# Join of the experts in a two-layer block: gated rows on VectorE and TensorE, two late experts

## The chip, the cores and the metric

One core of a Trainium2 chip runs the whole program; the other cores are idle. The metric is the device time of one execution in microseconds (us). The engines are named as in the profile: PE is TensorE's matmul stream and PEld its weight loads, DVE is VectorE, ACT is ScalarE, POOL is GpSimd, SP is the engine that issues most DMAs.

## What is computed

Two layers of a transformer block on 512 tokens of 1024 channels, in float32. Each layer has attention, a layer norm, a mixture of 16 experts of which every token uses two, and a second layer norm:

```python
x = layer_norm(ALPHA * x + mix, ln1_g[l], ln1_b[l])
ffn = grouped_moe(x, ...)       # sum over a token's two experts: gate * (silu(x Wg) * (x Wu)) Wd
x = layer_norm(ALPHA * x + ffn, ln2_g[l], ln2_b[l])
```

The change lies in the last two lines: how the expert rows of a token are added up, and the second layer norm on that sum.

## The kernel before

**Experts.** Each expert gets at most 128 of the tokens. `experts` runs over e = 0 to 15: it gathers the expert's tokens, transposes them, multiplies by the gate and up weights (`gate_up`) and, one step behind, by the down weights (`down(e - 1)` follows `gate_up(e)`). Float32 operands are split into a high and a low part (`granule`, lines L163 and L164: a cast on ScalarE and a subtraction on VectorE), and three products are summed. Weight tiles come through a pool of 12 buffers named `big`, loaded in program order by the queue of SP.

**Two ways for a result.** For an early expert ScalarE copies the result out of PSUM (L1102) and GpSimd scatters its rows, not yet gated, to a table in DRAM, `ydr`, with two rows per token (L1106). After all scatters SP loads the table back, one tile of 128 tokens at a time (`load_y`, L1217; the tiles are called `big<-ydr` in the trace and `ys[t]` in the code). The last `NJ` = 3 experts are the late ones, from `LATE` = 13 on: their results never go to DRAM. ScalarE and VectorE scale them by the gate and split them (L1095, L1096), and TensorE multiplies them with a transposed one-hot table `ohT`, which sends each row to its token. The table costs work inside `gate_up` of the expert before (`late_rows`: four transposes and four narrow matmuls L1122 on TensorE, a cast on each of GpSimd and ScalarE).

**Join.** `combine` then works on four tiles t = 0 to 3 of 128 tokens, tile `xs[t]` of 128 x 1024. For each it needs: two gated rows per token added (`add_y(t, a)`, a = 0, 1); the late experts' sum in PSUM (`join`, L1239, four matmuls per expert and tile); `mean`, which adds PSUM to the tile and sums it on VectorE (L1247, L1249) and squares it on ScalarE (L1251); `var`, a small VectorE step (L1255) and the inverse root on GpSimd (L185); `scale` (L1259) and two `finish` steps (L1264) on VectorE.

`add_y` has two forms. The plain one is a single VectorE instruction, y times gate plus x (L1227). With `two=True`, ScalarE scales (L1224) and GpSimd adds (L1225). Layer 0 uses the second form five times of eight, layer 1 two times of eight; in layer 1 tile 3 is added by TensorE, with the gates on a diagonal (`gates_of`, L1299, and `join_y`, L1306).

**What follows the join of layer 0.** TensorE transposes the finished tiles (`parts`, L190; ScalarE's cast L1273), and starts layer 1's input projection (L271) on tiles 0 and 1, the first half: 48 matmuls named `tr` and 48 named `mm`. Then `rest` transposes tiles 2 and 3, and the second half follows. The projection's first four weight granules are split within `combine` (`copy_w`, L1284 on ScalarE, and `sub_w`, L1289 on VectorE or GpSimd). In layer 1 (`last`) the finished halves are stored to the output by SP, and the program ends.

**Order.** Inside `combine` the order on each compute engine is the order in which the code is written (`manual_schedule`). Elsewhere a scheduler sets it. Every engine and SP's queue run their instructions in order, so one that waits holds all behind it.

Of the kernel before, what the change touches and what calls it, by code (L numbers as in the profile page):

```python
# [8 lines left out]
F32 = mybir.dt.float32  # L9
# [16 lines left out]
LOWER = 1500  # L26
NJ = 3
LATE = NE - NJ
# [67 lines left out]
def block_kernel(ctx, tc, xT0, x0, win, wqk, wuv, wo, gvec, lnp, rw, rb, wgu, wdn, consts, angles, stripd, rowsd, out):  # L96
# [915 lines left out]
    def experts(l, r, pre):  # L1012
# [126 lines left out]
        for e in range(NE):  # L1139
# [7 lines left out]
            if LATE - 1 <= e < NE - 1:  # L1147
                between[3] = lambda: late_rows(e + 1)
            if e == LATE + 1:
                between[3] = both(between[3], lambda: overflow(l, r))  # L1150
# [68 lines left out]

    def add_y(r, xs, t, a, two=False):  # L1220

        y, ga = r["ys"][t][:, a * D:(a + 1) * D], r["gates"][:, a * NT + t:a * NT + t + 1]
        if two:
            nc.scalar.activation(y, y, AF.Copy, scale=ga)  # L1224
            nc.gpsimd.tensor_add(xs[t], xs[t], y)  # L1225
        else:
            nc.vector.scalar_tensor_tensor(xs[t], y, ga, xs[t], op0=OP.mult, op1=OP.add)  # L1227

    def combine(l, r, y_parts, g, b, xs, win):
# [60 lines left out]

        def split_w(c, eng):
            copy_w(c)
            sub_w(c, eng)

        def gates_of(t):
# [12 lines left out]

        def normal(t):
            nr = sm.tile([128, 2], F32, name="cs")[:, 0:1]  # L1310
            nc.vector.tensor_mul(nr, nm[t], rs[t])
            nc.scalar.activation(xs[t], xs[t], AF.Identity, bias=nr, scale=rs[t])

        def gain(t):
            nc.vector.tensor_mul(xs[t], xs[t], g)  # L1315
            nc.gpsimd.tensor_add(xs[t], xs[t], b)  # L1316
            store(t)
# [36 lines left out]
        with tc.manual_schedule(engines={E.DVE, E.Pool, E.Activation, E.PE}):  # L1354
            add_y(r, xs, 0, 0, True)
            add_y(r, xs, 0, 1, True)
            add_y(r, xs, 1, 0)
            y_parts()
            join(0, 0, 1, 2)
            mean(0)  # L1360
            join(1, 0, 1, 2)
            add_y(r, xs, 1, 1)
            var(0)
            copy_w(0)
            sub_w(0, nc.gpsimd)
            mean(1)
            scale(0)
            join(2, 0, 1, 2)
            var(1)
            copy_w(1)  # L1370
            add_y(r, xs, 2, 0, True)
            finish(0, 0)
            finish(0, 1)
            parts(0, 0)
            parts(0, 1)
            add_y(r, xs, 2, 1, True)
            join(3, 0, 1)
            scale(1)
            finish(1, 0)
            finish(1, 1)  # L1380
            small(0, 0)
            small(0, 1)
            parts(1, 0)
            parts(1, 1)
            join(3, 2)
            add_y(r, xs, 3, 0, True)
            small(1, 0)
            small(1, 1)
            sub_w(1)
            copy_w(2)  # L1390
# [9 lines left out]
            sub_w(3, nc.gpsimd)  # L1400
            var(3)
            finish(2, 0)
            finish(2, 1)
            scale(3)
            finish(3, 0)
            finish(3, 1)
# [95 lines left out]
```

## Time and profile before

| what | value |
|---|---|
| time, median of 3 runs | 1199.4 us (1197.04, 1199.4, 2881.24) |
| time of the profiled execution | 1201.73 us |
| its span in the trace | 1199.9 us |
| PE busy, share of the span | 95% |
| join of layer 0 up to the first projection matmul | about 575 to 597 us |
| second half of layer 1's projection | 614 to 627 us |
| join of layer 1, to the end | about 1169 to 1200 us |

The profiled execution took 1201.73 us, of which 1199.9 us lie between its first and its last recorded instruction. Times within it are us from the start of the span. A row of the timeline gives start, duration, engine, line, operation, output and inputs, and how many instructions are merged in it; in brackets the idle time before it and what ended that. The lines are those of the kernel printed above.

### The profile page before, as it was taken

What the parts mean: (1) busy time and instruction counts of PE and PEld (TensorE: products, weight loads), DVE (VectorE), ACT (ScalarE), POOL (GpSimd) and SP (SyncE); (2) the same over time, 40 slices, a digit from 0 to 9 for tenths busy, and PEclk for the clock granted to TensorE, in tenths of its full rate; (3) what the DMA queues carried; (4) which work ended last, traced back from release to release, by engine and by line L of the source; (5) the groups of instructions that cost most, each with busy time, mean ns of one, the idle gap of its engine ahead of it and who ended that gap; (6) DMA issues with size and microseconds to landing.
All of it is one profiled execution on the core that took longest, in us unless ns stands there. A gap on an engine that the chain in (4) does not pass through costs nothing. (4 is left out here: it accounts for less than half of the span.)

```text
span 1199.9 us, 16838 instructions
## 1 busy us (share of the span) xinstructions
PE 1144.9 (95%) x5737; PEld 897.3 (75%) x5737; DVE 1026.7 (86%) x1859; ACT 802.0 (67%) x1264; POOL 303.4 (25%) x241
## 2 busy tenths in 40 slices
PE   8999899999999999999898998999999999999995
PEld 6686555788788888887686865567887888888873
DVE  4599967399999999988957999773999999999897
ACT  4633668445888888888645246683468888888882
POOL 2335233121211111210542353422212111111004
PEclk8999999999999999999999999999999999999998
DMA  7626104366999999998235270144669999999841
GB/s 248 195 81 207 66 1 141 140 245 251 403 395 396 392 386 372 371 330 310 86 124 156 67 252 8 40 140 155 248 269 396 401 390 386 396 376 367 307 176 70
DMA packets 56971, 292.20 MB, mean 244 GB/s; under 512 B 10063, under 2 KB 13903, under 8 KB 28464
## 3 DMA queue, kind: packets, MB, share of 16 engines
q1 hardware_dynamic: 47376, 270.48, 60.7%
q0 software_dynamic: 8064, 15.36, 3.5%
q10 hardware_dynamic: 1440, 5.24, 1.1%
q8 instruction: 46, 0.75, 0.3%
q14 instruction: 45, 0.37, 0.1%
HBM read 267.96 MB, written 31.98 MB: 250 GB/s over the span
## 5 line engine op out<-in xcount | busy, mean ns | idle before, releaser
L163 ACT CAST hl<-big 128x1024 fp32r<-128x1024 f32 x438 | 457.2, 1054 | 125.6 <-PE mm L1065 51.6
L164 DVE TENSOR_TENSOR hl<-big,hl 128x1024 fp32r<-128x1024 f32 x403 | 483.6, 1226 | 48.4 <-ACT hl L163 41.7
L1064 PE MATMUL mm<-hl,xh 128*128 128x512 f32 x504 | 207.3, 411 | 0.6 <-ACT hl L163 0.6
L1065 PE MATMUL mm<-hl,xh 128*128 128x512 f32 x504 | 197.2, 391 | 0.0
L1086 PE MATMUL pv<-hl,hT 128*128 128x512 f32 x720 | 169.9, 390 | 0.1
L1086 PEld LDWEIGHTS pv<-hl,hT 128*128 128x128 f32 x720 | 134.7, 188 | 28.8 <-DVE hl L164 1.0
L271 PE MATMUL mm<-big,hl 128*128 128x512 f32 (+1 forms) x624 | 142.5, 387 | 2.7 <-ACT hl L163 1.4
L271 PEld LDWEIGHTS mm<-big,hl 128*128 128x128 f32 x624 | 114.2, 195 | 28.5 <-ACT hl L163 3.3
L1028 POOL DMA_INDIRECT xg<-xdr,ii x30 | 53.9, 1796 | 263.5 <-DVE ii L1042 237.1
L164 POOL TENSOR_TENSOR hl<-big,hl 128x1024 fp32r<-128x1024 f32 x35 | 85.7, 2453 | 136.5 <-ACT hl L163 122.2
L1064 PEld LDWEIGHTS mm<-hl,xh 128*128 128x128 f32 x504 | 94.8, 188 | 16.7 <-ACT hl L163 1.1
L1065 PEld LDWEIGHTS mm<-hl,xh 128*128 128x128 f32 x504 | 95.0, 189 | 15.5
L1065 PE MATMUL mm<-hl,xl 128*128 128x512 f32 x252 | 98.8, 392 | 0.0
L1064 PE MATMUL mm<-hl,xl 128*128 128x512 f32 x252 | 98.7, 392 | 0.0
L635 PE MATMUL mm<-hl,big 128*128 128x512 f32 x384 | 93.3, 395 | 0.0
L492 ACT ACTIVATE P<-P,mn 128x128 f32<-128x128 f32 (+3 forms) x128 | 71.9, 569 | 18.6 <-DVE mn L490 16.5
L635 PEld LDWEIGHTS mm<-hl,big 128*128 128x128 f32 x384 | 70.8, 188 | 13.6
L504 ACT COPY big<-tr 128x512 f32<-128x512 f32 (+3 forms) x128 | 49.7, 431 | 36.5 <-PE tr L502 35.5
L502 PE MATMUL tr<-cn,P 128*128 128x128 f32 x320 | 61.8, 293 | 9.8 <-DVE P L498 9.2
L502 PEld LDWEIGHTS tr<-cn,P 128*128 128x128 f32 x320 | 36.0, 141 | 42.8 <-ACT big L504 16.8
L1106 POOL DMA_INDIRECT ydr<-y,ii x26 | 28.2, 1085 | 149.8 <-ACT y L1102 112.5
L572 POOL TENSOR_TENSOR mh<-dd,cn 128x256 f32<-128x256 f32 (+2 forms) x64 | 44.5, 717 | 66.1 <-DVE mn L490 39.8
(279 smaller groups left out, 1857.7 us busy)
## 6 DMA issues: line engine op xcount, KB each, us to landing
big<-wgu SPq DMA_DIRECT2D x128, 1024.0 KB, 8.4
big<-wdn SPq DMA_DIRECT2D x64, 1024.0 KB, 7.8
big<-win SPq DMA_DIRECT2D x10, 1024.0 KB, 5.6
ydr<-zz SPq DMA_DIRECT2D x2, 4096.0 KB
big<-wo SPq DMA_DIRECT2D x8, 1024.0 KB, 14.0
big<-ydr SPq DMA_DIRECT2D x8, 1024.0 KB, 5.0
big<-wqk SPq DMA_DIRECT2D x4, 1024.0 KB, 4.9
big<-dq SPq DMA_DIRECT2D x32, 128.0 KB, 2.3
```

The lines of the kernel that those rows point to most:

```text
L163: i = nc.scalar.copy(hi, src).ins
L164: last_lo[0] = (eng or nc.vector).tensor_sub(lo, src, hi.bitcast(F32)).ins
L271: nc.tensor.matmul(p[:, ts], w[j == 1][:, k * 128:(k + 1) * 128], x, start=(j + k == 0), stop=(j == end and k == 7))
L492: nc.scalar.activation(e, e, AF.Exp, bias=mn[:, i:i + 1], scale=-1.0, accum_out=su[:, i:i + 1])
L502: nc.tensor.transpose(p[:, (i - kb) * 128:(i - kb + 1) * 128], P[:, PO[i] + kb * 128:PO[i] + (kb + 1) * 128], ident)
L504: copies.append(nc.scalar.copy(pt[kb], p[:, :512 - 128 * kb]).ins)
L572: last_mask[0] = nc.gpsimd.tensor_tensor(m[:, c:c + w], dd, C("slope", h, h + 1).to_broadcast([128, w]), op=OP.mult)
L635: R["pe"] = nc.tensor.matmul(pp[t][i], x, w[:, i * 512:(i + 1) * 512], start=first, stop=last).ins
L1028: return nc.gpsimd.indirect_dma_start(out=st[e]["xg"], out_offset=None, in_=xdr[l], in_offset=bass.IndirectOffsetOnAxis(ap=st[e]["ii"][:, ...
L1064: nc.tensor.matmul(pg, x, w[:, :512], start=(k == 0 and x is a and w is wh), stop=last)
L1065: nc.tensor.matmul(pu, x, w[:, 512:], start=(k == 0 and x is a and w is wh), stop=last)
L1086: nc.tensor.matmul(py[i], x, w[:, i * 512:(i + 1) * 512], start=(k == 0 and x is a and w is wh), stop=last)
```

## The change

`NJ` falls from 3 to 2, so expert 13 becomes an early one: its rows are scattered to `ydr` and its one-hot table is not made. All `add_y` calls are single VectorE instructions, and they are made for tiles 0 and 1 alone. In both layers tiles 2 and 3 get their gated rows from TensorE (`gates_of`, `join_y`). The sums of tiles 0 and 1 (`mean(0)`, `mean(1)`) both stand ahead of `scale(0)`. In layer 1 `normal` and `gain`, which used GpSimd for the last addition, are gone, and all four tiles use `scale` and `finish`. The computed function is the same.

```diff
-NJ = 3
+NJ = 2
...
-            if e == LATE + 1:
+            if e == NE - 2:
                 between[3] = both(between[3], lambda: overflow(l, r))
...
-    def add_y(r, xs, t, a, two=False):
+    def add_y(r, xs, t, a):
 
         y, ga = r["ys"][t][:, a * D:(a + 1) * D], r["gates"][:, a * NT + t:a * NT + t + 1]
-        if two:
-            nc.scalar.activation(y, y, AF.Copy, scale=ga)
-            nc.gpsimd.tensor_add(xs[t], xs[t], y)
-        else:
-            nc.vector.scalar_tensor_tensor(xs[t], y, ga, xs[t], op0=OP.mult, op1=OP.add)
+        nc.vector.scalar_tensor_tensor(xs[t], y, ga, xs[t], op0=OP.mult, op1=OP.add)
...
-                                     stop=(e == NJ - 1 and j == 1 and not (last and t == 3)))
+                                     stop=(e == NJ - 1 and j == 1 and t < 2))
...
+        jj = range(NJ)
+
         if last:
             with tc.manual_schedule(engines={E.DVE, E.Pool, E.Activation, E.PE}):
-                d3 = gates_of(3)
-                add_y(r, xs, 0, 0, True)
-                add_y(r, xs, 0, 1, True)
+                d = {t: gates_of(t) for t in (2, 3)}
+                add_y(r, xs, 0, 0)
+                add_y(r, xs, 0, 1)
                 add_y(r, xs, 1, 0)
+                join(0, *jj[:-1])
+                join(1, *jj[:-1])
                 y_parts()
-                join(0, 0, 1, 2)
+                join(0, jj[-1])
+                join(1, jj[-1])
+                add_y(r, xs, 1, 1)
                 mean(0)
-                join(1, 0, 1, 2)
-                add_y(r, xs, 1, 1)
+                mean(1)
                 var(0)
-                mean(1)
-                join(2, 0, 1, 2)
-                join(3, 0, 1, 2)
-                add_y(r, xs, 2, 0)
-                normal(0)
+                join(2, *jj)
+                join_y(2, d[2])
+                scale(0)
                 var(1)
-                add_y(r, xs, 2, 1)
-                normal(1)
-                gain(0)
+                finish(0, 0)
+                finish(0, 1)
                 mean(2)
-                join_y(3, d3)
-                gain(1)
+                scale(1)
+                join(3, *jj)
+                join_y(3, d[3])
+                finish(1, 0)
+                finish(1, 1)
+                mean(3)
                 var(2)
                 scale(2)
-                mean(3)
...
         with tc.manual_schedule(engines={E.DVE, E.Pool, E.Activation, E.PE}):
-            add_y(r, xs, 0, 0, True)
-            add_y(r, xs, 0, 1, True)
+            d = {t: gates_of(t) for t in (3, 2)}
+            add_y(r, xs, 0, 0)
+            add_y(r, xs, 0, 1)
             add_y(r, xs, 1, 0)
+            join(0, *jj[:-1])
+            join(1, *jj[:-1])
             y_parts()
...
+            for c in range(3):
+                copy_w(c)
+            join(0, jj[-1])
+            join(1, jj[-1])
+            add_y(r, xs, 1, 1)
             mean(0)
...
+            mean(1)
             var(0)
...
+            join(3, *jj)
+            join_y(3, d[3])
             scale(0)
...
+            join(2, *jj)
             finish(1, 0)
             finish(1, 1)
...
+            join_y(2, d[2])
             copy_w(3)
+            sub_w(2, nc.gpsimd)
+            for t in range(2):
+                for i in range(2):
+                    small(t, i)
             store(0)
             store(1)
-            sub_w(2, nc.gpsimd)
+            sub_w(0)
+            sub_w(1)
+            sub_w(3)
             mean(2)
-            add_y(r, xs, 3, 1)
+            mean(3)
             var(2)
-            mean(3)
             scale(2)
```

In the changed file the lines have other numbers: L1223 is the VectorE form of `add_y`, L1235 `join`, L1243 and L1245 `mean`, L1251 `var`, L1285 `sub_w`, L1291 `gates_of`, L1298 `join_y`.

TensorE's row in the join of layer 0, from the last expert's down product (L1086) to the first projection matmuls (L271); `dg` is the diagonal of gates. Before:

```order
L1086 MATMUL mm<-hl,hT 128x512 x24
L1239 MATMUL mm<-big,ohT 128x512 x12
L1239 MATMUL pv<-big,ohT 128x512 x24
L190 MATMUL tr<-cn,x_2196 128x128 x8
L1239 MATMUL mm<-big,ohT 128x512 x8
L190 MATMUL mm<-cn,x_2259 128x128 x8
L1239 MATMUL mm<-big,ohT 128x512 x4
L271 MATMUL tr<-big,hl 128x256 x48
```

And now:

```order
L1235 MATMUL mm<-big,ohT 128x512 x4
L1235 MATMUL pv<-big,ohT 128x512 x4
L1235 MATMUL mm<-big,ohT 128x512 x4
L1235 MATMUL pv<-big,ohT 128x512 x4
L1235 MATMUL mm<-big,ohT 128x512 x8
L1298 MATMUL mm<-big,dg 128x512 x4
L190 MATMUL tr<-cn,x_2196 128x128 x8
L1235 MATMUL pv<-big,ohT 128x512 x8
L190 MATMUL mm<-cn,x_2259 128x128 x8
L1298 MATMUL pv<-big,dg 128x512 x4
L271 MATMUL tr<-big,hl 128x256 x48
```

48 join matmuls became 32, and two groups of four with the gates' diagonal came in; the second group stands directly ahead of the projection.

VectorE's row in the same place, from the first gated rows on; x_2196 and x_2259 are tiles 0 and 1. Before:

```order
L1227 SCALAR_TENSOR_TENSOR x_2259<-big,r_gates,x_2259 128x1024
L1096 SCALAR_TENSOR_TENSOR big<-mm,gs,big 128x512 x2
L1247 SCALAR_TENSOR_TENSOR x_2196,cs<-mm,x_2196 128x512 x2
L1249 TENSOR_SCALAR cnm<-cs 128x1
L1255 TENSOR_SCALAR cv<-cq 128x1
L1247 SCALAR_TENSOR_TENSOR x_2259,cs<-pv,x_2259 128x512 x2
L1259 SCALAR_TENSOR_TENSOR x_2196<-x_2196,cnm,lnp 128x1024
```

And now:

```order
L1223 SCALAR_TENSOR_TENSOR x_2196<-big,r_gates,x_2196 128x1024 x2
L1223 SCALAR_TENSOR_TENSOR x_2259<-big,r_gates,x_2259 128x1024
L1096 SCALAR_TENSOR_TENSOR big<-mm,gs,big 128x512 x2
L1243 SCALAR_TENSOR_TENSOR x_2196,cs<-mm,x_2196 128x512 x2
L1243 SCALAR_TENSOR_TENSOR x_2259,cs<-pv,x_2259 128x512 x2
L1251 TENSOR_SCALAR cv<-cq 128x1
L1255 SCALAR_TENSOR_TENSOR x_2196<-x_2196,cnm,lnp 128x1024
```

Rows that stand twice are shown once. Tile 0's two gated rows now come from VectorE, ahead of the last expert's low parts (L1096), and both sums precede the first scaling.

GpSimd's row in the same place, up to the next attention's first split (L164). Before:

```order
L1225 TENSOR_TENSOR x_2196<-x_2196,big 128x1024 x2
L185 TENSOR_TENSOR cly<-cv,mhalf 128x1
L1289 TENSOR_TENSOR hl<-big,hl 128x1024
L1225 TENSOR_TENSOR x_2421<-x_2421,big 128x1024 x2
L1225 TENSOR_TENSOR x_2500<-x_2500,big 128x1024
L164 TENSOR_TENSOR hl<-big,hl 128x1024 x5
```

And now:

```order
L1106 DMA ydr_85<-y,ii 1024x1024
L1291 TENSOR_TENSOR dg<-cn,r_gates 128x128 x4
L185 TENSOR_TENSOR cly<-cv,mhalf 128x1 x2
L1285 TENSOR_TENSOR hl<-big,hl 128x1024
L185 TENSOR_TENSOR cly<-cv,mhalf 128x1 x2
L164 TENSOR_TENSOR hl<-big,hl 128x1024 x5
```

Here too a row that stands twice is shown once. Of eight operations on full tiles (five additions and three weight subtractions) one subtraction is left, and expert 13's scatter and the four diagonals stand ahead of it.

## Rows read from the trace of the kernel before

**Rows 1.** The page: busy time by engine (part 1), ScalarE's full-tile cast (part 5).
```profile
PE 1144.9 (95%) x5737; PEld 897.3 (75%) x5737; DVE 1026.7 (86%) x1859; ACT 802.0 (67%) x1264; POOL 303.4 (25%) x241
...
L163 ACT CAST hl<-big 128x1024 fp32r<-128x1024 f32 x438 | 457.2, 1054 | 125.6 <-PE mm L1065 51.6
```
**Rows 2.** Stretches, join of layer 0: length, busy PE, PEld, DVE, ACT, POOL; PEclk, DMA, GB/s.
```profile
585.00:590.00 5.00, 2.85 (x14) 1.92 (x12) 4.96 (x4) 3.71 (x5) 3.77 (x3) 1.00 0.56 188
...
610.00:615.00 5.00, 3.60 (x19) 2.90 (x18) 4.87 (x7) 2.14 (x4) 0.00 (x0) 0.74 0.35 143
```
**Rows 3.** Timeline, GpSimd: the scatters of experts 9 to 12 in layer 0.
```profile
478.20 1.01 POOL L1106 DMA_INDIRECT ydr<-y,ii  x1 [4.93 <-DVE hl L164]
...
496.12 1.01 POOL L1106 DMA_INDIRECT ydr<-y,ii  x1 [4.88 <-ACT y L1102]
...
515.38 1.01 POOL L1106 DMA_INDIRECT ydr<-y,ii  x1 [4.90 <-ACT y L1102]
...
534.44 0.98 POOL L1106 DMA_INDIRECT ydr<-y,ii  x1 [13.71 <-DVE hl L164]
```
**Rows 4.** Timeline, join of layer 0 and layer 1's first projection, all engines.
```profile
553.77 1.27 ACT L1095 ACTIVATE big<-pv,gs 128x512 fp32r<-128x512 f32 x2
...
574.58 3.42 DVE L1227 SCALAR_TENSOR_TENSOR x<-big,r_gates,x 128x1024 f32<-128x1024 f32 x1
...
587.79 3.52 DVE L1264 SCALAR_TENSOR_TENSOR x<-x,cly,lnp 128x512 f32<-128x512 f32 x2
...
588.36 2.41 POOL L1225 TENSOR_TENSOR x<-x,big 128x1024 f32<-128x1024 f32 x1
588.71 0.63 PE L190 MATMUL tr<-cn,x 128*128 128x128 f32 x4 [1.49 <-DVE x L1264]
...
591.84 3.66 PE L1239 MATMUL mm<-big,ohT 128*128 128x512 f32 x8
...
597.13 5.92 PE L271 MATMUL tr<-big,hl 128*128 128x256 f32 x48
...
611.70 1.42 DVE L1264 SCALAR_TENSOR_TENSOR x<-x,cly,lnp 128x512 f32<-128x512 f32 x2
...
614.30 1.89 PE L271 MATMUL tr<-big,hl 128*128 128x256 f32 x8
...
621.79 4.96 PE L271 MATMUL mm<-big,hl 128*128 128x256 f32 x40
```
**Rows 5.** One stretch of 1 us in layer 0's join, columns as in rows 2.
```profile
592.00:593.00 1.00, 1.00 (x4) 0.81 (x4) 0.90 (x2) 0.87 (x2) 0.00 (x0) 0.50 0.00 0
```
**Rows 6.** Timelines by engine, join of layer 1: VectorE, GpSimd, TensorE.
```profile
1169.15 3.42 DVE L1227 SCALAR_TENSOR_TENSOR x<-big,r_gates,x 128x1024 f32<-128x1024 f32 x1
...
1174.86 0.69 DVE L1247 SCALAR_TENSOR_TENSOR x<-mm,x 128x512 f32<-128x512 f32 x1 [0.96 <-POOL x L1225]
...
1176.33 1.27 DVE L1227 SCALAR_TENSOR_TENSOR x<-big,r_gates,x 128x1024 f32<-128x1024 f32 x1
...
1194.47 1.41 DVE L1264 SCALAR_TENSOR_TENSOR x<-x,cly,lnp 128x512 f32<-128x512 f32 x2 [0.44 <-POOL cly L185]
...
1180.98 1.51 POOL L185 TENSOR_TENSOR cly<-cv,mhalf 128x1 f32<-128x1 f32 x1 [2.39 <-DVE cv L1255]
...
1174.29 2.91 PE L1239 MATMUL pv<-big,ohT 128*128 128x512 f32 x12
...
1182.48 3.59 PE L1306 MATMUL mm<-big,dg 128*128 128x512 f32 x8
```
**Rows 7.** One line's instructions, L1106 (the scatters): from issue to landing.
```profile
DMA to landing us min/median/max: 3.2/8.5/10.0
```
**Rows 8.** One line's instructions, L1217 (the y loads, 1 MB each): from issue to landing.
```profile
DMA to landing us min/median/max: 4.9/5.0/5.0
```
**Rows 9.** Two stretches near the end of layer 0's experts, columns as in rows 2.
```profile
555.00:560.00 5.00, 5.00 (x26) 4.15 (x25) 5.00 (x7) 4.51 (x7) 0.00 (x0) 1.00 1.02 374
...
565.00:570.00 5.00, 5.00 (x26) 4.13 (x25) 4.93 (x5) 4.27 (x7) 0.00 (x0) 1.00 0.76 281
```

More of the change, by code (lines that the diff above doesn't have):

```diff
@@ L1289, in sub_w @@
             eng.tensor_sub(lo, src, hi.bitcast(F32))
-        def split_w(c, eng):
-            copy_w(c)
-            sub_w(c, eng)
         def gates_of(t):
@@ L1307, in join_y @@
                                      ys[t][:, a * D + i * 512:a * D + (i + 1) * 512], start=False, stop=(a == 1))
[L1309 to L1317, printed above, removed]
         E = mybir.EngineType
+        jj = range(NJ)
         if last:
             with tc.manual_schedule(engines={E.DVE, E.Pool, E.Activation, E.PE}):
-                d3 = gates_of(3)
-                add_y(r, xs, 0, 0, True)
-                add_y(r, xs, 0, 1, True)
+                d = {t: gates_of(t) for t in (2, 3)}
+                add_y(r, xs, 0, 0)
+                add_y(r, xs, 0, 1)
                 add_y(r, xs, 1, 0)
+                join(0, *jj[:-1])
+                join(1, *jj[:-1])
                 y_parts()
-                join(0, 0, 1, 2)
+                join(0, jj[-1])
+                join(1, jj[-1])
+                add_y(r, xs, 1, 1)
                 mean(0)
-                join(1, 0, 1, 2)
-                add_y(r, xs, 1, 1)
+                mean(1)
                 var(0)
-                mean(1)
-                join(2, 0, 1, 2)
-                join(3, 0, 1, 2)
-                add_y(r, xs, 2, 0)
-                normal(0)
+                join(2, *jj)
+                join_y(2, d[2])
+                scale(0)
                 var(1)
-                add_y(r, xs, 2, 1)
-                normal(1)
-                gain(0)
+                finish(0, 0)
+                finish(0, 1)
                 mean(2)
-                join_y(3, d3)
-                gain(1)
+                scale(1)
[4 more added lines that the diff above has]
+                mean(3)
                 var(2)
                 scale(2)
-                mean(3)
                 finish(2, 0)
@@ L1354, in combine @@
         with tc.manual_schedule(engines={E.DVE, E.Pool, E.Activation, E.PE}):
-            add_y(r, xs, 0, 0, True)
-            add_y(r, xs, 0, 1, True)
+            d = {t: gates_of(t) for t in (3, 2)}
+            add_y(r, xs, 0, 0)
+            add_y(r, xs, 0, 1)
             add_y(r, xs, 1, 0)
+            join(0, *jj[:-1])
+            join(1, *jj[:-1])
             y_parts()
-            join(0, 0, 1, 2)
+            for c in range(3):
[3 more added lines that the diff above has]
+            add_y(r, xs, 1, 1)
             mean(0)
-            join(1, 0, 1, 2)
-            add_y(r, xs, 1, 1)
+            mean(1)
             var(0)
-            copy_w(0)
-            sub_w(0, nc.gpsimd)
-            mean(1)
+            join(3, *jj)
+            join_y(3, d[3])
             scale(0)
-            join(2, 0, 1, 2)
             var(1)
-            copy_w(1)
-            add_y(r, xs, 2, 0, True)
             finish(0, 0)
@@ L1375, in combine @@
             parts(0, 1)
-            add_y(r, xs, 2, 1, True)
-            join(3, 0, 1)
             scale(1)
+            join(2, *jj)
             finish(1, 0)
             finish(1, 1)
-            small(0, 0)
-            small(0, 1)
             parts(1, 0)
             parts(1, 1)
[L1385 to L1390, printed above, removed]
+            join_y(2, d[2])
             copy_w(3)
+            sub_w(2, nc.gpsimd)
+            for t in range(2):
+                for i in range(2):
+                    small(t, i)
             store(0)
             store(1)
-            sub_w(2, nc.gpsimd)
+            sub_w(0)
+            sub_w(1)
+            sub_w(3)
             mean(2)
-            add_y(r, xs, 3, 1)
+            mean(3)
             var(2)
-            mean(3)
             scale(2)
-            sub_w(3, nc.gpsimd)
-            var(3)
             finish(2, 0)
             finish(2, 1)
+            var(3)
             scale(3)
```

## The prediction

> **What bounds the kernel now.** I read the page first. TensorE is busy 95% of the span [rows 1], so the time can only fall where TensorE is idle, where its clock is low, or where it has less to do. Next I cut the joins into stretches. From 585 to 590 us TensorE is busy 2.85 of 5 us and from 610 to 615 us 3.60, while VectorE has 4.96 and 4.87 [rows 2]: here VectorE sets the pace. Soon after such a gap the granted clock is 0.50, the lower level of 1.2 GHz [rows 5], and eight join matmuls take 3.66 us [rows 4] where twelve took 2.91 at full clock [rows 6]. At the end of layer 1 nothing follows the join, so its VectorE chain is the end of the program. Last I read the timelines for why VectorE is slow. The same gated addition takes 3.42 us [rows 4, 6] or 1.27 us [rows 6]; a pair of `finish` steps takes 3.52 us while a GpSimd addition of 2.41 us runs, and 1.42 us without [rows 4]. So a full-tile GpSimd operation in the join is paid for on VectorE.
>
> The Trainium skill says the same more strictly ("SBUF — State Buffer", "SBUF: two separate sides"): GpSimd and a VectorE operation with two SBUF inputs share one port pair under an exclusive lock. It speaks against what is left on GpSimd: the one `sub_w(2)` and the inverse roots would still stop VectorE for their whole length. By its rule the stop is 2.41 us, by the rows 3.52 - 1.42 = 2.1; the sum would move by 0.3 us.
>
> **Part one, two late experts.** Scatters follow each other by 17.92 us where the expert ahead has no `late_rows` (478.20 to 496.12), and by 19.26 and 19.06 us where it has (515.38, 534.44) [rows 3]. TensorE is full there, so each `late_rows` costs 1.14 to 1.34 us. One goes in each layer: 2 x 1.2 = 2.4 us, range 2.3 to 2.7. Expert 13 swaps ScalarE's scaled casts for plain copies of the same size, and VectorE loses two steps there: nothing, since TensorE sets the pace.
>
> New is a wait. The y loads stand behind expert 13's scatter. ScalarE reads that result at 553.77 [rows 4], the scatter goes out about 1.3 us later, and landing takes 3.2 us at best [rows 7]. Then SP's queue runs: a first load takes 5.0 us [rows 8], so the first y tile is there at 553.8 + 1.3 + 3.2 + 5.0 = 563.3, eleven us before VectorE wants it at 574.6 [rows 4]. Behind it in SP's queue are three y tiles, two norm parameters (half size) and two tiles of weights: six tiles of 1.05 MB in all, at 374 GB/s [rows 9] 16.8 us, so that the last, the weight tile of `copy_w(2)`, lands about 580.1. On ScalarE that cast (1.05 us, [rows 1]) now stands ahead of the squares of tiles 0 and 1. They are wanted at 582.1 (below), so the tile may land as late as 581. I take nothing for it, with 1 us of slack; the bounds are nothing and what rival B works out.
>
> **Part two, the join of layer 0.** I walk the new order in the times of before. Lengths, start to start: a full-tile step 1.2 us (1.27 less the overlap), a mean 1.47 (1174.86 to 1176.33), a `finish` pair 1.4, the root behind a `scale` 0.44 of wait [rows 6].
>
> - VectorE: from 574.6 three additions, 3.6 us, to 578.2. Before, one addition held it until 578.0, because GpSimd was at work [rows 4]; so the extra work is free up to here. The last expert's low parts 1.3, the fourth addition 1.2, to 580.7. Two means 2.9, to 583.6; `var` and `scale` 1.3, root 0.44, to 585.4. `finish(0)` 1.4, plus 2.1 for `sub_w(2)`, which is next on GpSimd just then: 588.9. `scale(1)` and `finish(1)`: 591.5.
> - TensorE: joins of tiles 0, 1, 3 and the first diagonal group fill its time to about 586; then tile 0's transposes and the join of tile 2 lie inside VectorE's `finish` steps. After 591.5 come the last transposes, 0.63 [rows 4], and the second diagonal group, 3.59 [rows 6]: the projection starts at 595.7. Before it was 597.13 [rows 4]. The diagonal thus eats most of what VectorE gave here.
> - First half: 96 matmuls at 4.96/40 = 0.124 us [rows 4], 11.9 us, to 607.6. VectorE meanwhile has four half and three full weight-side steps, two means, two scales and finishes: 4 x 0.7 + 3 x 1.2 + 2 x 1.47 + 2 x 1.3 + 2 x 1.85 = 15.6 us from 591.5, done at 607.1, before 607.6. Before, its last `finish` ended at 613.1 [rows 4], and TensorE waited: this is the main gain.
> - Then 16 transposes at 0.63 per four, 2.5 us, and a short wait for casts: the second half starts at 610.3 against 614.30, and without the low clock of before (eight matmuls in 1.89 us, [rows 4]) takes 11.9 us: end 622.2 against 621.79 + 4.96 = 626.75.
>
> Gain 4.5 us. If `sub_w(2)` finds a gap, 6.6. All that follows in layer 1's attention hangs on this point, so it moves along.
>
> The cost of a diagonal group in layer 0 is not shown before, only layer 1's: 3.59 us at full clock; at the lower level it would double, to 7.2. I take 3.59, the nearest row.
>
> **Part three, the join of layer 1.** VectorE from 1169.15 [rows 6], same steps: three additions, low parts, the fourth addition, two means, to 1178.2; `scale(0)` and root 1179.9; `finish(0)` 1181.3; mean(2) 1182.8; `scale(1)`, `finish(1)` 1185.4. TensorE: the low parts are ready at 1174.0, then 8 join matmuls at 2.91/12 = 0.24 (1.9 us), tile 2's 8 and its diagonal (1.9 + 3.6), tile 3's the same: 1186.6. So mean(3) waits 0.5 us for TensorE and ends at 1187.4; `var`, `scale(2)` and root 1189.1, `finish(2)` 1190.5, the same for tile 3 1.75, `finish(3)` 1.4: 1193.7, against 1194.47 + 1.41 = 1195.9 before [rows 6]. Gain 2.2 us; 3.5 if no root waits and mean(3) doesn't. The stores after it are of the same form as before.
>
> **Sum.** 2.4 + 4.5 + 2.2 = 9.1 us. The profiled execution took 1201.7, so its like would take 1192.6. It stood 2.3 us above the median of the runs; from the median, 1199.4 - 9.1 = 1190.3 us.
>
> **The rivals.**
>
> A. TensorE becomes the bound of layer 0's join, at the lower clock. Before, the level fell after the gaps of 585 to 592 us [rows 2, 5]. In the new order one gap stays, between tile 0's and tile 1's transposes. If the level falls, the diagonal group of tile 2 costs 3.6 us more and the start of the projection 1.5 more: layer 0 gives -0.6, the whole 4.0 us, 1195.4. For it: the gap lies just ahead. Against it: TensorE is full for the ten us before, where it was not. The Trainium skill ("TensorE: Matmul & The Clock Gate", "What's actually happening") ties the level to how busy the engine has been lately, which favours no fall; no run here shows the new mix. Chance 0.22.
>
> B. The other side, slower: the loads behind the last scatter come late, in layer 0. Place: `copy_w(2)` on ScalarE, which holds up both squares and so `var(0)`. Each us past 581 costs one. With the median landing of 8.5 us [rows 7] the tile lands at 585.4, which costs 4.4: layer 0 gives 0.1 and the time is 1194.7. With the longest landing, 10.0, and 281 GB/s [rows 9] instead of 374, it lands 6.8 + 5.6 us later, at 592.5: layer 0 gives 4.5 - 11.5 = -7.0, and the time is 1199.4 - 2.4 + 7.0 - 2.2 = 1201.8. It decides at 590: beyond, the kernel is slower than before. For it: the loads now wait for a scatter that comes a whole expert later than the last one did. Against: at 555 the queue is empty, since all expert weights have been issued, and an empty queue gives the short landing. Chance 0.18 that it costs over 1 us, 0.05 that it ends slower.
>
> C. VectorE is freer than I walk it: `sub_w(2)` slips into a wait and the roots cost nothing. Then 2.7 + 6.6 + 3.5 = 12.8 us, 1186.6. For it: a root's 1.51 us [rows 6] depends on what VectorE does at that moment. Against: GpSimd's row puts it directly behind the second root. Chance 0.1.
>
> **How the numbers follow.** My walk has 0.5, A 0.22, B 0.18, C 0.1. The prediction is the walk's 1190.3. The range reaches down past C by the spread of the runs, to 1185, and up past A and the milder B to 1199; the slower part of B is left out. A measurement of this kernel tells about 2%, 24 us, from no change. No case reaches that downwards, and upwards only B would with far later loads: faster 0.02, same 0.95, slower 0.03.
>
> **What would show it.** Right: `add_y` at 1.2 to 1.3 us each and no VectorE step over 2 us in the joins but one; y loads issued about 559 and tile `copy_w(2)` there by 581; first projection matmul about 0.2 us after the second diagonal group; no wait of TensorE for VectorE at the transposes of tiles 2 and 3; scatters of experts 11 and 12 17.9 and 19.2 us behind the one before each. Wrong: a granted clock of 0.50 between 590 and 600 us (A), ScalarE idle on a load ahead of the squares (B), or a join that begins late because the first y tile is missing.

## The result, and the profile of the changed kernel

The changed kernel took 1192.4 us (median of 7 runs, 1190.8 to 1196.5) against 1199.7 us for the kernel before: a ratio of 0.9931, 95% interval 0.9918 to 0.9945, or 6.6 to 9.8 us. The ratio is that of the fast runs alone, without the one run of the kernel before that took 2881 us; the two medians as they stand differ by 7.3 us. The profiled execution took 1192.6 us with a span of 1190.8; before it was 1201.7 with 1199.9. The forecast was 1190.3 us, by a gain of 9.1. The two traces also differ by 9.1 us of span, but 1.1 us of that lies ahead of the first changed instruction and is no part of the change, so that this agreement to the tenth is luck.

The busy times of the page answer to [rows 1]. TensorE is busy 2.3 us less, VectorE 6.5 us less (a step that is stopped counts as busy):

```profile
PE 1142.6 (96%) x5705; PEld 893.5 (75%) x5705; DVE 1020.2 (86%) x1858; ACT 791.2 (66%) x1253; POOL 285.6 (24%) x236
```

The timeline of GpSimd in the changed kernel shows the scatters of experts 9 to 13, to be read beside [rows 3]. The third one now follows the second after 17.95 us instead of 19.26: a `late_rows` is gone. The fourth still has one ahead of it, 19.12. The fifth is new; the y loads wait for it.

```profile
477.10 1.01 POOL L1106 DMA_INDIRECT ydr<-y,ii  x1 [4.93 <-ACT y L1102]
...
495.02 1.01 POOL L1106 DMA_INDIRECT ydr<-y,ii  x1 [4.93 <-ACT y L1102]
...
512.97 1.01 POOL L1106 DMA_INDIRECT ydr<-y,ii  x1 [4.91 <-ACT y L1102]
...
532.09 0.99 POOL L1106 DMA_INDIRECT ydr<-y,ii  x1 [13.78 <-DVE hl L164]
...
552.81 0.97 POOL L1106 DMA_INDIRECT ydr<-y,ii  x1 [19.73 <-DVE hl L164]
```

The join of layer 0 in the changed kernel follows, as rows of the timelines of VectorE, ScalarE, GpSimd and TensorE (start, length, and in brackets the idle time ahead and what ended it). They answer to [rows 4].

```profile
572.27 3.80 DVE L1223 SCALAR_TENSOR_TENSOR x<-big,r_gates,x 128x1024 f32<-128x1024 f32 x3
...
583.25 3.51 DVE L1260 SCALAR_TENSOR_TENSOR x<-x,cly,lnp 128x512 f32<-128x512 f32 x2 [0.26 <-POOL cly L185]
...
588.05 1.41 DVE L1260 SCALAR_TENSOR_TENSOR x<-x,cly,lnp 128x512 f32<-128x512 f32 x2
...
604.46 1.42 DVE L1260 SCALAR_TENSOR_TENSOR x<-x,cly,lnp 128x512 f32<-128x512 f32 x2 [0.44 <-POOL cly L185]
...
575.34 2.94 ACT L1280 CAST hl<-big 128x1024 fp32r<-128x1024 f32 x3
...
583.72 2.49 POOL L1285 TENSOR_TENSOR hl<-big,hl 128x1024 fp32r<-128x1024 f32 x1
...
578.71 1.98 PE L1235 MATMUL mm<-big,ohT 128*128 128x512 f32 x8
...
584.15 0.63 PE L190 MATMUL tr<-cn,x 128*128 128x128 f32 x4
...
586.90 1.09 PE L190 MATMUL tr<-cn,x 128*128 128x128 f32 x4 [2.12 <-DVE x L1260]
587.64 3.27 PE L1235 MATMUL pv<-big,ohT 128*128 128x512 f32 x8
...
590.75 1.03 PE L190 MATMUL mm<-cn,x 128*128 128x128 f32 x8
...
591.62 3.60 PE L1298 MATMUL pv<-big,dg 128*128 128x512 f32 x8
594.65 6.31 PE L271 MATMUL tr<-big,hl 128*128 128x256 f32 x48
...
608.82 6.01 PE L271 MATMUL tr<-big,hl 128*128 128x256 f32 x48 [0.34 <-ACT big L1269]
614.66 5.92 PE L271 MATMUL mm<-big,hl 128*128 128x256 f32 x48
```

Three additions take 3.80 us where one took 3.42. The one GpSimd step left, `sub_w(2)` (L1285), falls on `finish(0)` (L1260) and makes it 3.51 us. TensorE then waits 2.12 us for the second half of `finish(0)`. The eight join matmuls behind that gap take 3.27 us; eight of the same form at 578.71 (L1235 into `mm`) take 1.98. The waits for VectorE at tiles 2 and 3 are gone: the second half of the projection waits 0.34 us, for a cast of ScalarE, and VectorE's last `finish` is done at 605.88, ahead of TensorE's transposes of tiles 2 and 3.

The stretches of the changed kernel (columns as in [rows 2]) say the same. The low clock, level 1.2 GHz, is still there, but in one place (587 to 590 us) instead of the two of before ([rows 5], and the 0.74 of [rows 2]).

```profile
585.00:590.00 5.00, 3.10 (x10) 2.65 (x11) 4.90 (x6) 0.99 (x2) 1.21 (x1) 0.68 0.65 246
605.00:610.00 5.00, 4.66 (x41) 4.42 (x40) 3.05 (x6) 2.06 (x4) 0.00 (x0) 1.00 0.26 107
610.00:615.00 5.00, 5.00 (x44) 5.00 (x43) 0.78 (x2) 1.10 (x2) 0.00 (x0) 1.00 0.00 0
...
588.00:589.00 1.00, 1.00 (x3) 0.78 (x3) 0.94 (x2) 0.59 (x1) 0.00 (x0) 0.50 0.53 221
...
591.00:592.00 1.00, 1.00 (x9) 0.81 (x7) 0.00 (x0) 0.62 (x2) 0.00 (x0) 1.00 0.62 139
```

The join of layer 1 (VectorE, then TensorE), beside [rows 6]: `mean(3)` (L1243 at 1178.76) starts directly behind `finish(1)`, and the last `finish` ends at 1186.59.

```profile
1162.28 3.80 DVE L1223 SCALAR_TENSOR_TENSOR x<-big,r_gates,x 128x1024 f32<-128x1024 f32 x3
...
1178.76 0.68 DVE L1243 SCALAR_TENSOR_TENSOR x<-mm,x 128x512 f32<-128x512 f32 x1
...
1185.18 1.41 DVE L1260 SCALAR_TENSOR_TENSOR x<-x,cly,lnp 128x512 f32<-128x512 f32 x2 [0.44 <-POOL cly L185]
...
1175.80 3.59 PE L1298 MATMUL mm<-big,dg 128*128 128x512 f32 x8
```

The y loads (L1217) now run in one burst, with the weight tiles (L228) among and behind them. The trace above has a landing on record for only two of its eight y loads ([rows 8] for three of eight), so these times are from the second trace of the same kernel (experiment 5), layer 0: the four y loads, then the two weight tiles, from issue to landing.

```profile
DMA to landing us min/median/max: 4.9/10.0/14.7
...
DMA to landing us min/median/max: 10.8/13.8/16.8
```

The first load takes 4.9 us, as one did before ([rows 8]); each one behind it in the queue lands later.

**Stages.** A single run of this kernel moves by 2 or 3 us for reasons outside the joins. Over the traces below the scatter of expert 9, ahead of any changed instruction, starts anywhere from 475.2 to 478.4, and the attention of layer 1 takes 285.1 to 286.7. So the lengths of the stages between fixed instructions are compared, as differences of two starts in one trace. "To the join" is from the scatter of expert 9 (before any difference) to VectorE's first gated addition of layer 0; "join 0" from there to the first matmul of L315, which follows the projection; "experts 1" from layer 1's first scatter to its first gated addition; "join 1" from there to the end of the last `finish`.

| kernel | to the join | join 0 | experts 1 | join 1 |
|---|---|---|---|---|
| before | 96.38 | 52.10 | 257.22 | 26.73 |
| changed | 95.17 | 48.24 | 256.03 | 24.31 |
| changed, second trace | 95.18 | 48.28 | 256.02 | 24.30 |
| before, two late experts | 95.18 | 51.86 | 256.02 | 26.70 |
| changed, three late experts | 96.37 | 47.61 | 257.22 | 27.06 |
| before, additions all on VectorE | 96.38 | 50.11 and 48.62 | 257.22 | 26.06 and 26.05 |
| changed, one late expert | 99.17 | 57.03 | 261.42 | 24.25 |
| changed, `sub_w(2)` on VectorE | 95.17 | 44.91 | 256.02 | 24.29 |
| changed, `sub_w(2)` later on GpSimd | 95.17 | 44.98 | 256.03 | 24.31 |
| changed, TensorE's order | 95.17 | 46.18 | 256.03 | 24.29 |
| `sub_w(2)` on VectorE, `var` ahead | 95.17 | 44.92 | 256.03 | 23.59 |

By stages the change gave 1.21 + 3.86 + 1.19 + 2.42 = 8.7 us. The attention of layer 1 took back 0.5 in the profiled execution.

### The profile page after: what moved, and what is told of

It is laid out like the page before. It is cut to its first block, busy times and chain, and to the rows that moved or that the text cites. A ratio compares the mean times of both kernels' runs of the same rounds, so it can differ in the third digit from the quotient of the medians.

```text
span 1190.8 us, 16760 instructions
## 1 busy us (share of the span) xinstructions
PE 1142.6 (96%) x5705; PEld 893.5 (75%) x5705; DVE 1020.2 (86%) x1858; ACT 791.2 (66%) x1253; POOL 285.6 (24%) x236
## 5 line engine op out<-in xcount | busy, mean ns | idle before, releaser
L164 DVE TENSOR_TENSOR hl<-big,hl 128x1024 fp32r<-128x1024 f32 x403 | 483.7, 1227 | 47.7 <-ACT hl L163 41.7
L1086 PE MATMUL pv<-hl,hT 128*128 128x512 f32 x720 | 169.9, 390 | 0.1
L1086 PEld LDWEIGHTS pv<-hl,hT 128*128 128x128 f32 x720 | 134.7, 188 | 28.7 <-DVE hl L164 1.0
L271 PE MATMUL mm<-big,hl 128*128 128x512 f32 (+1 forms) x624 | 140.3, 384 | 2.4 <-ACT big L163 1.7
L271 PEld LDWEIGHTS mm<-big,hl 128*128 128x128 f32 x624 | 112.9, 193 | 27.7 <-ACT hl L163 2.3
L164 POOL TENSOR_TENSOR hl<-big,hl 128x1024 fp32r<-128x1024 f32 x35 | 86.5, 2476 | 133.7 <-ACT hl L163 118.2
L1064 PEld LDWEIGHTS mm<-hl,xh 128*128 128x128 f32 x504 | 94.8, 188 | 16.8 <-ACT hl L163 1.1
L1106 POOL DMA_INDIRECT ydr<-y,ii x28 | 30.2, 1079 | 189.4 <-ACT y L1102 117.5
```

The costliest lines, as they stand in the source:

```text
L164: last_lo[0] = (eng or nc.vector).tensor_sub(lo, src, hi.bitcast(F32)).ins
L271: nc.tensor.matmul(p[:, ts], w[j == 1][:, k * 128:(k + 1) * 128], x, start=(j + k == 0), stop=(j == end and k == 7))
L1064: nc.tensor.matmul(pg, x, w[:, :512], start=(k == 0 and x is a and w is wh), stop=last)
L1086: nc.tensor.matmul(py[i], x, w[:, i * 512:(i + 1) * 512], start=(k == 0 and x is a and w is wh), stop=last)
```

## The experiments

**1. Three late experts in the changed kernel.** The edit undoes part one:

```diff
-NJ = 2
+NJ = 3
```

> The changed kernel with three late experts again, all else as changed. My theory: the third late_rows comes back in each layer, 1.2 us each on a full TensorE, so the scatter of expert 12 to 13's distance shows 19.1 us where the changed kernel has 17.95 for the expert ahead of it; the third expert's 16 join matmuls per layer fill gaps for the tiles 0 to 2 and cost about 1 us for tile 3 in each join: 2 x 1.2 + 2 x 1.0 = 4.4 us more than the changed kernel's 1192.4, 1196.8. Rival: late_rows lies in gaps of TensorE and the gain came from the joins alone: 1192.4 to 1194.4, with the same pitch of the scatters.

Measured 1195.3 us, ratio 0.9957 (0.9944 to 0.9970), that is 3.1 us above the changed kernel by the ratios. The two expert stages give back 1.20 and 1.19 us, as expected of a full TensorE. The matmuls are another matter. In join 0 sixteen more of them made the stage 0.63 us *shorter*: they push tile 0's transposes back into the stopped `finish(0)`, so the gap ahead of the second group is 0.49 us and the clock stays at 1.00. In join 1 they cost 2.75 us: TensorE reaches the ends of the diagonals of tiles 2 and 3 late, and `mean(2)` waits 0.7 us in its two halves, `mean(3)` 1.8. Rows of this kernel, TensorE in layer 0, then VectorE in layer 1:

```profile
586.33 0.63 PE L190 MATMUL tr<-cn,x 128*128 128x128 f32 x4 [0.49 <-DVE x L1260]
...
1181.14 0.69 DVE L1243 SCALAR_TENSOR_TENSOR x<-mm,x 128x512 f32<-128x512 f32 x1 [1.64 <-PE mm L1298]
```

**2. Two late experts in the kernel before.** Part one alone:

```diff
-NJ = 3
+NJ = 2
...
-            if e == LATE + 1:
+            if e == NE - 2:
...
-            join(3, 0, 1)
+            join(3, 0)
...
-            join(3, 2)
+            join(3, 1)
```

The other calls of `join` name one expert fewer.

> The kernel before with two late experts, and nothing else changed. Theory: only the two late_rows go, 1.2 us each, because VectorE sets the pace of both joins before and the third expert's matmuls lie in TensorE's idle time: 1200.3 - 2.4 = 1197.9, with the stretch from the first gated addition to the last finish of layer 1 within 0.5 us of before's 26.7. Rival: as in the changed kernel with three late experts, where they cost layer 1's join 2.75 us, the matmuls that go count too: 1200.3 - 2.4 - 2.8 = 1195.1. A second rival is that the rows, scattered an expert later, hold up the first gated addition: over 1200.

Measured 1199.2 us, with the kernel before at 1201.3 beside it, ratio 0.9979 (0.9968 to 0.9990), 1.2 to 3.8 us less. The stages: 1.20 and 1.20 us from `late_rows`, 0.24 from join 0, 0.03 from join 1. The first theory holds and the second rival falls: rows scattered an expert later do not hold up the first addition. With experiment 1 this shows an interaction. In join 1 neither part gives anything alone (two late experts 0.03, the new order with three -0.33); together they give 2.42, because the new order puts two diagonal groups on TensorE and only has room for them where an expert's matmuls are gone.

**3. Every gated addition on VectorE in the kernel before.** GpSimd's additions go, and with them ScalarE's scaling ahead of each; nothing else:

```diff
-            add_y(r, xs, 0, 0, True)
-            add_y(r, xs, 0, 1, True)
+            add_y(r, xs, 0, 0)
+            add_y(r, xs, 0, 1)
```

and the same for the other five calls with `True`.

> The kernel before with every gated addition as one step on VectorE, and nothing else changed: no GpSimd additions, no second diagonal group, three late experts. Theory (GpSimd's full-tile additions cost VectorE more than the steps themselves): in layer 0 VectorE is rid of about 9.4 us of stops and has five steps of 1.2 us more, net 3.4 us less, in layer 1 two steps more against stops of 2.2 us and a join of tile 0 that begins earlier, about 1 us less: 1199.4 - 4.4 = 1195.0. Rival: it is the diagonal on TensorE, that is less work on VectorE, that gave the gain; then VectorE's 6 us and 2.4 us of added steps show in full where it sets the pace: 1199.4 to 1204.

Measured 1198.6 us, ratio 0.9976 (0.9965 to 0.9987), 2.9 us less. Join 0 is 2.0 us shorter although VectorE has five full-tile steps more, join 1 is 0.7 shorter with two more. The rival falls: with its scaling, its stop and the waits for its result, an addition on GpSimd cost the join more than VectorE's own step. Which of the three weighs most is not told apart here. The size was less than the 4.4 expected, and join 0 of this kernel has two lengths; the next experiment shows where they part.

**4. The same kernel again.** No edit.

> The kernel before with every gated addition on VectorE once more, in every line the same, for the clock alone: in its first trace TensorE's gap of 2.5 us near 586 us was followed by a granted clock of 1.00. If what the work is decides, it is 1.00 again; if it is a matter of the single execution, 0.50 can appear for some us behind the gap, and the join takes up to 2 us more. Time 1198 to 1201 in either case.

Measured 1195.0 us (one run), where the runs of experiment 3 had a median of 1198.6 (1194.7 to 1200.0). Behind the gap near 586 us the clock was 1.00 again. But join 0 took 48.62 us instead of 50.11, and the 1.49 us lie in one place: the start of the projection's second half, where the first trace has the level of 1.2 GHz and the second does not. In both, TensorE had just waited 0.74 and 1.40 us for VectorE (0.73 and 1.40 in the second). First trace, then second, TensorE's timeline:

```profile
608.99 1.32 PE L190 MATMUL mm<-cn,x 128*128 128x128 f32 x8 [1.40 <-DVE x L1264]
610.33 1.78 PE L271 MATMUL tr<-big,hl 128*128 128x256 f32 x8
611.90 1.91 PE L271 MATMUL mm<-big,hl 128*128 128x256 f32 x8
```

```profile
607.55 1.32 PE L190 MATMUL mm<-cn,x 128*128 128x128 f32 x8 [1.40 <-DVE x L1264]
608.88 1.21 PE L271 MATMUL tr<-big,hl 128*128 128x256 f32 x8
609.93 1.12 PE L271 MATMUL mm<-big,hl 128*128 128x256 f32 x8
```

So the same work behind the same waits fell to the lower level in one execution and not in the other. The Trainium skill ("TensorE: Matmul & The Clock Gate", "What's actually happening") says that the chip's look at the engine's activity does not start with the kernel, so that one kernel can differ between runs. These two traces do differ, by 1.49 us; that this is the reason is not shown here.

**5. The changed kernel again.** No edit.

> The changed kernel once more, in every line the same, to see what of its trace repeats. Theory: VectorE's stop beside GpSimd's sub_w(2) (finish(0) 3.5 us) and TensorE's gap of 2.1 us come from the order and are there again, and the clock falls to 0.50 behind the gap again, since the same work stands ahead of it: projection start 22.4 us behind the first gated addition, 1192.0. Rival: whether the clock falls behind a gap of this size is not fixed (in the kernel with every addition on VectorE a gap of 2.5 us was followed by 1.00); then the gap is there with a clock of 1.00 behind it, the start comes 1.3 us sooner, and the time of single runs is spread by as much.

Measured 1193.8 us, ratio 0.9935 (0.9917 to 0.9952). The trace repeats: `finish(0)` is stopped, the gap is 2.12 us, the clock falls to 0.50 behind it, the projection starts 22.42 us behind the first addition, and every stage is within 0.04 us of the first trace. The rival is not seen in these two traces.

**6. `sub_w(2)` on VectorE in the changed kernel.**

```diff
             copy_w(3)
-            sub_w(2, nc.gpsimd)
...
             sub_w(1)
+            sub_w(2)
             sub_w(3)
```

> The changed kernel with the weight step sub_w(2) on VectorE, behind sub_w(1), instead of on GpSimd. Theory: GpSimd's 2.49 us subtraction stops VectorE's finish(0) pair for its whole length, and so made TensorE's gap and the low clock behind it. Without it the pair takes 1.4 us instead of 3.51, the gap of 2.1 us ahead of tile 0's second transposes goes, the granted clock between 587 and 590 us is 1.00 instead of 0.50, and the projection starts about 2.3 us earlier; VectorE gives 1.2 us of it back for the step itself, so its last finish ends 0.9 us earlier and the second half of the projection ends 0.9 to 2.0 us earlier: 1190.4 to 1191.5. Rival: the finish pair is long for another reason (its own operands or the root's result that comes late); it then stays at 3.5 us, the clock falls as before, VectorE has 1.2 us more and the time is 1192.4 to 1193.6.

Measured 1190.2 us, ratio 0.9917 (0.9904 to 0.9930). Join 0 is 3.33 us shorter, more than the 0.9 to 2.0 expected. All parts of the theory are in the rows: `finish(0)` takes 1.42 us, tile 0's eight transposes run in one piece, the clock is 1.00 from 583 to 595 us, and the projection starts 18.75 us behind the first addition instead of 22.38.

```profile
583.11 1.42 DVE L1260 SCALAR_TENSOR_TENSOR x<-x,cly,lnp 128x512 f32<-128x512 f32 x2 [0.26 <-POOL cly L185]
...
584.00 1.29 PE L190 MATMUL tr<-cn,x 128*128 128x128 f32 x8
585.05 2.10 PE L1235 MATMUL pv<-big,ohT 128*128 128x512 f32 x8
...
590.89 6.32 PE L271 MATMUL tr<-big,hl 128*128 128x256 f32 x48
```

What I had missed: VectorE's low parts of tile 1 had themselves waited 1.33 us for a cast that came late because TensorE was late. That wait goes too and pays for the step that VectorE took over; its last `finish` ends 2.4 us earlier.

**7. TensorE's order alone.** GpSimd's step stays where it is; the gap is filled with work that was there:

```diff
             parts(0, 0)
+            join(2, *jj)
             parts(0, 1)
             scale(1)
-            join(2, *jj)
+            join_y(2, d[2], 0)
...
             parts(1, 1)
-            join_y(2, d[2])
+            join_y(2, d[2], 1)
```

The third argument of `join_y` takes one of its two gated rows.

> The changed kernel with TensorE's order in layer 0's join changed: the eight join matmuls of tile 2 between tile 0's two groups of transposes, and half of tile 2's diagonal group ahead of tile 1's transposes. GpSimd's step stays. Theory: the gap of 2.1 us on TensorE ahead of tile 0's second transposes is filled, the clock stays at 1.00 from 584 to 592 us, the eight join matmuls take 1.95 us instead of 3.27, and the projection starts 2.0 us earlier; its second half waits for VectorE's finish(3), which does not move, so that the end moves by 1.0 to 1.5 us: 1191.1. Rival: the clock falls for another reason than the gap (the transposes themselves, or the mix of work), then the order changes nothing but the place of the low clock: 1192.0 to 1192.8.

Measured 1188.4 us, ratio 0.9896 (0.9881 to 0.9910). `finish(0)` is still 3.55 us, but the join matmuls take 2.09 us in the place of the gap and the projection starts 19.09 us behind the first addition. Join 0 is 2.06 us shorter. With VectorE as late as before at this point, this shows by itself what the gap and the low clock, together, cost on TensorE. The median is below that of experiment 6, but join 0 is longer than there by 1.27 us, and the attention of layer 1 alone moves by more than 1.5 us from trace to trace: the medians do not order these two kernels, the stages do.

```profile
584.85 2.09 PE L1235 MATMUL pv<-big,ohT 128*128 128x512 f32 x8
...
588.00:589.00 1.00, 1.00 (x3) 0.38 (x2) 0.90 (x2) 0.51 (x1) 0.00 (x0) 1.00 1.03 336
```

**8. `sub_w(2)` on GpSimd, beside steps that read PSUM.** The step waits for the second low part of tile 0 (the third argument of `sub_w` adds that wait):

```diff
+                    if (t, i) == (1, 0):
+                        sub_w(2, nc.gpsimd, late)
-                    small(t, i)
+                    late = small(t, i)
```

> The changed kernel with sub_w(2) left on GpSimd, but held back until VectorE's second low part of tile 0 (L1275) is done, so that it runs beside VectorE's steps that read one operand from PSUM (the low parts of tile 1) instead of beside finish(0). Theory A: only VectorE's steps with both tensors in SBUF are stopped; the two low parts of tile 1 then take 1.3 us as before, finish(0) 1.4 us, TensorE's gap goes, and the projection starts 18.8 us behind the first gated addition, as with the step on VectorE; the end of the projection 44.9 us behind it, time 1189 to 1191. Theory B: every VectorE step is stopped; the pair of low parts takes 3.5 us. TensorE is not held by it, so the start is the same 18.8, and VectorE's later steps are 1 to 2 us later: 1189 to 1192. The pair's duration tells the two apart, not the time.

Measured 1190.5 us, ratio 0.9904 (0.9885 to 0.9924); join 0 44.98 us. Theory A: the two low parts of tile 1, one operand in PSUM, take 1.28 us under GpSimd's step. The three weight steps behind them, both operands in SBUF, take 4.68 us for three instead of 3.49: they are held until GpSimd is done at 592.01. VectorE's rows, then GpSimd's:

```profile
589.49 1.28 DVE L1275 TENSOR_TENSOR big<-mm,big 128x512 fp32r<-128x512 f32 x2
590.69 4.68 DVE L1285 TENSOR_TENSOR hl<-big,hl 128x1024 fp32r<-128x1024 f32 x3
...
589.65 2.36 POOL L1285 TENSOR_TENSOR hl<-big,hl 128x1024 fp32r<-128x1024 f32 x1 [4.92 <-DVE big L1275]
```

The Trainium skill ("SBUF — State Buffer", "SBUF: two separate sides") names just this: of VectorE's ordinary steps those with two SBUF inputs share the port pair with GpSimd, and the loser stops until the other ends. The trace agrees, with 1.28 us for the one kind and 1.19 us more for the other.

**9. One late expert.** Rival B of the prediction, made to happen:

```diff
-NJ = 2
+NJ = 1
```

> The changed kernel with one late expert. The scatter of expert 14 then stands ahead of the y loads and goes out about 17 us later than that of expert 13 does now, near 570 us. Theory (rival B of the prediction, decided): landing takes 2.6 to 10 us and the first load 5 to 10.6 us more, so that the first y tile is there between 577 and 591 us where VectorE wants it at 571, and the join of each layer begins 6 to 19 us late; two more late_rows less give 2.4 back: 1192.4 - 2.4 + (12 to 38) = 1202 to 1228, I take 1212. Rival (the loads are hidden anyway): 1190.0, or less by what the sixteen matmuls fewer give.

Measured 1210.7 us, ratio 1.0076 (1.0048 to 1.0104): slower than before. Rows of VectorE (layer 0, then layer 1), ScalarE and TensorE:

```profile
576.92 2.60 DVE L1223 SCALAR_TENSOR_TENSOR x<-big,r_gates,x 128x1024 f32<-128x1024 f32 x2 [5.44 <-DMA big<-ydr]
...
595.70 0.15 DVE L1251 TENSOR_SCALAR cv<-cq 128x1 f32<-128x1 f32 x1 [8.89 <-ACT big L1247]
...
1180.43 3.80 DVE L1223 SCALAR_TENSOR_TENSOR x<-big,r_gates,x 128x1024 f32<-128x1024 f32 x3 [6.86 <-DMA big<-ydr]
...
593.48 1.04 ACT L1280 CAST hl<-big 128x1024 fp32r<-128x1024 f32 x1 [5.54 <-DMA big<-win]
...
590.99 5.63 PE L1298 MATMUL mm<-big,dg 128*128 128x512 f32 x8 [3.86 <-DMA big<-ydr]
```

The join itself begins 4.0 us late in layer 0 and 5.4 in layer 1, because the first y tile is not there. The rest of layer 0's loss is in the place that rival B named: ScalarE's third weight cast waits for the last weight tile, both squares stand behind it, and VectorE's `var(0)` waits 8.89 us for them. (TensorE's diagonal group, 5.63 us and in part at 1.2 GHz, lies under that wait.) In the changed kernel the three casts run in one piece from 575.34 (above): the slack was there, and one expert later it is overdrawn.

**10. A version that beats both.** `sub_w(2)` on VectorE, and in layer 1's join the roots taken under other work:

```diff
                 finish(1, 0)
+                var(2)
                 finish(1, 1)
                 mean(3)
-                var(2)
                 scale(2)
                 finish(2, 0)
+                var(3)
                 finish(2, 1)
-                var(3)
                 scale(3)
```

> The changed kernel with sub_w(2) on VectorE, as in the run before of that name, and in layer 1's join the var steps ahead, so that the inverse root of tile 2 is taken under finish(1) and mean(3) and that of tile 3 under finish(2): VectorE's two waits of 0.44 us for GpSimd's roots (tiles 2 and 3) go. Theory: 0.9 us less in layer 1's join (24.3 to 23.4 us from the first gated addition to the end of the last finish), 0.9 us less than the 1190.2 of sub_w(2) alone, 1189.3. Rival: the root beside VectorE's two-operand steps takes longer than 1.45 us, or the squares come late for the earlier var, and the waits only move: 1190.2 to 1191.

Measured 1188.2 us, ratio 0.9891 (0.9871 to 0.9911), 13 us less than before by the ratio; against experiments 6 and 7 the times alone tell nothing. Join 1 is 0.72 us shorter than in the changed kernel. Both waits of 0.44 us are gone (the rows of VectorE's last two steps carry no idle time); the rest of the 0.88 is paid for the two small steps, which now part pairs of `finish`. GpSimd's root takes 0.92 us under them, not 1.45.

```profile
1178.19 0.92 POOL L185 TENSOR_TENSOR cly<-cv,mhalf 128x1 f32<-128x1 f32 x1 [3.33 <-DVE cv L1251]
...
1178.63 1.28 DVE L1255 SCALAR_TENSOR_TENSOR x<-x,cnm,lnp 128x1024 f32<-128x1024 f32 x1
1180.01 1.42 DVE L1260 SCALAR_TENSOR_TENSOR x<-x,cly,lnp 128x512 f32<-128x512 f32 x2
```

## Why the prediction was right, and where it was off

**Right in the sum and in its terms.** By stages: `late_rows` 2.4 forecast, 1.21 + 1.19 measured; join 0 4.5 and 3.86; join 1 2.2 and 2.42. Experiments 1 and 2 show the first term by itself, in both kernels, at 1.2 us each.

**Join 0, the step that was mis-sized.** The working let TensorE start the projection 1.4 us earlier, at 595.7 in the times of before. Put into those times (the first addition lies 2.31 us earlier now) it started at 596.96: 0.2 us earlier than before, and 1.3 us later than forecast. The stop of `finish(0)` by `sub_w(2)` was in the working, on VectorE: 3.5 us, as measured. The step that failed is "tile 0's transposes and the join of tile 2 lie inside VectorE's `finish` steps": TensorE stands in the middle of that stop, between tile 0's two groups of transposes, with nothing queued that could run. Its gap is 2.1 us, and the eight join matmuls behind it ran at 1.2 GHz (3.27 us instead of 1.98). So tile 1's transposes start at 590.75, 1.3 us after `finish(1)` has ended (588.05 + 1.41). The sum had no term for the gap or for the low clock; rival A had one for the clock, in another place. Experiments 6 and 7 take the stop away, or fill the gap, and both get the time back. From the start of the projection on the walk was good: the second half began at 611.1 (forecast 610.3) and ended at 622.9 (622.2), with no wait for VectorE at tiles 2 and 3.

**Rival A was half of what happened.** The clock did fall in this stretch, and the sign that the working gave for it (0.50 between 590 and 600) is there at its start (589.1 to 592.5 in the times of before), but over the join matmuls of tile 2 and one group of transposes. The diagonal group behind them took 3.60 us, full clock, where the rival wanted 7.2; so the cost was about 1.3 us on the join matmuls, and not the 5.1 of the rival's two items. The argument against a fall, that TensorE had been full for ten us, did not hold: it had been busy from 574.2 to 584.8 but for one wait of 0.38 us, and behind the gap of 2.12 us the clock fell, in both traces.

**"If `sub_w(2)` finds a gap, 6.6"**: experiment 8 gives it one (it still stops VectorE there, for 1.2 us), experiment 6 takes it off GpSimd, and join 0 is 7.1 and 7.2 us shorter than before.

**Rival B had the place right, and the slack was larger than the working's.** The first y tile took 4.9 us, and the loads behind it landed one after another, the weight tile of `copy_w(2)` 16.8 us after its issue. In the second trace that is at 576.9, or 578.9 in the times of before, where 580.1 was forecast. The third cast did not wait for it: it started at 577.5, when the second was done, and could have started as late as 579.3 (the first square at 580.3, less the cast's 1.05). So the slack was 2.4 us where the working took 1. Experiment 9 moves the scatter by one expert and the forecast wait appears on ScalarE. There the third cast starts some 14 us after the point where it would hold up the squares (580.1 us in the changed kernel, less the cast's 1.05), and layer 0's two stages are 12.8 us longer: about one us for each, as the rival had it.

**Join 1 was right for a reason that the working gave only in part.** It credited the new order of VectorE with 2.2 us and let `mean(3)` wait 0.5 for TensorE; it waited for nothing (0.06 us between its halves). Two sums of this part slipped: by its own terms TensorE ends at 1186.9 and not 1186.6, and the gain with no wait at all, which rival C uses, is 4.0 us and not 3.5. Experiments 1 and 2 show that the gain needs the missing expert as much as the new order.

## What to carry to other kernels

Before moving work from a busy engine to an idle one, look at what the two share: here one full-tile step of 2.4 us on GpSimd stopped VectorE's steps with two operands in SBUF for 2.1 us, and VectorE did the same step itself in 1.2. Steps with an operand in PSUM were not stopped (experiment 8). When a step is stopped, ask which engine stands behind its middle, not only its end: the 2.1 us stop cost more on TensorE, in a gap and a lower clock behind it, than on the engine that was stopped. Two parts of a change can each be worth nothing alone and 2.4 us together, as in join 1, so undo them one at a time from both ends.

## What was not expected of the hardware

- The granted clock is not settled by the work: one kernel had 0.50 at 611 us in one execution and 1.00 in the other behind the same waits of 0.74 and 1.40 us, a difference of 1.49 us. Over two traces each, a gap of 2.1 us was followed by the lower level in the changed kernel and one of 2.5 us by the upper in the kernel of experiments 3 and 4. Why the longer gap left the clock alone stays open.
- GpSimd's root of a 128x1 column took 1.45 us beside `scale` and 0.92 us beside halves of `finish`. In both it ended 0.40 us after VectorE's step (601.30 after 600.90 in the changed kernel, 1179.11 after 1178.71 in experiment 10), and beside a step with an operand in PSUM it took 0.57 us (583.45 in the kernel before). So GpSimd waits for VectorE as VectorE does for GpSimd; that it is the same port pair was not tried by itself.
